# Residual added inside the second FFN product, the first product's last block in another order, and the final norm by halves of the tokens, in a one-core float32 decoder layer

## The chip, the core and the metric

The kernel runs on one core of a Trainium2 chip. The metric is the device time of one execution in microseconds (us), smaller being better. The core's engines are named as in the profile: PE is TensorE, DVE is VectorE, ACT is ScalarE, POOL is GpSimd and SP is SyncE. Each works through its own queue in order; waits between engines are semaphores. DMAs are issued from the queue of SP, POOL or ACT and land some microseconds later.

## The reference, cut to what matters

The program computes one layer for 512 prompt tokens and 8 sample tokens, T = 520 token columns, with 2048 features and 8192 FFN features, all in float32. The change touches everything from the residual of the mixers on:

```python
    x = x + jnp.einsum('blm,md->bld', mix, p['w_out'][l].astype(x.dtype))
    hf = rms_norm(x, p['norm_ffn'][l])
    ff = jnp.square(jax.nn.relu(jnp.einsum('bld,df->blf', hf, p['w_ff1'][l].astype(x.dtype))))
    x = x + jnp.einsum('blf,fd->bld', ff, p['w_ff2'][l].astype(x.dtype))
...
    y = rms_norm(x, p['norm_final'])
```

`rms_norm` divides by the root of the mean square over the features, plus 1e-6, and multiplies by a vector.

## The kernel before, in words

**Layout.** Features lie on the 128 partitions and the 520 tokens along the free axis. Tokens are taken in two halves of H = 260 columns, here called c0 and c1. One 128x128 weight block times 260 columns in float32 is done as three matmuls: weights and operands are each split into a high part that PE multiplies in its fast 32-bit form and a low rest (high by high, high by low, low by high). For weights ACT makes the high part (`whi`, L1064) and DVE the rest (`wlo`, L1066).

**Stages.** The in-projection, the mixers and the out-projection take until about 583 us of the span. Then comes FFN1, 32 quads (of 2x2 block groups) with 8 blocks along the inner dimension, about 20 us each. Then FFN2, whose inner dimension of 32 operand groups is cut into windows: 44 quads, of which the first eight have 3, 4, 5, 6, 7, 7, 7 and 7 blocks, and the last eight 6, 6, 6, 6, 7, 7, 7 and 7, and then 5, 4, 3 and 2 for the last pair groups in their last window. Each pass over the windows adds onto 16 result tiles, `X`.

**Quads.** A quad needs not eight products of weight halves by token halves but seven, P1, P2, P3, Q4, P5, P6, P7, on sums and differences of weights (DVE, `sums`, L1028, tiles `raw`) and of operands (`T` and `G` tiles). Each product is an item. Items stand in one list: P1 of a quad, P3 of the quad before, P2, Q4 of the quad before, P6, P7, P5. At item k, PE multiplies item k (`product`) and DVE and ACT make the sums and splits of item k+3 (`split_item`, AHEAD = 3). So what DVE or ACT does late for one item stops PE three items on. `after(n, f)` puts a function into a later item.

**FFN1's results.** `ff1_done` turns the products of quad i into the four operands that FFN2 reads for group i (relu, square, sums; `first_hi`, `hi_of`, `lo_of`), and `store` writes their seven tiles to DRAM (`fx<-o`, L906, on POOL's queue). Since FFN1's input operands fill SBUF until P5 of quad 31 is done, `more_operands` loads FFN2's operands (`o<-fx`, L1019, POOL's queue) as tiles come free; `budget` counts those. In the same list of loads stand the 16 tiles of the residual, `X<-x1d` (L1013, POOL's queue): the two `X` tiles of a window are loaded before its operands, and four items later DVE multiplies each with S2 (`scale_x`, L1000), a row of scale factors. Then P1, P2, P3 (L926) and P7, P5, Q4 (L929) of the window add onto them.

**Norms.** `hf_half` forms the FFN input per half block while the out-projection runs; it also squares the tile on ACT and adds the square to a sum on DVE (`square`, L417; `ssum`, L423 and L425). After item 2 of FFN1 a matmul with ones (`side_sum`, L1111) turns these sums into S2. At the end `sq` does the same for the 16 finished tiles of X, `rstd` (L285 to L289) makes the factor with Ln and Exp on ACT and three operations on DVE, per token half, and a loop (L1217, L1218) multiplies each X tile, 520 columns wide, and stores it (16 DMAs, on SP and ACT).

Of the kernel before, what the change touches and what calls it, by code (L numbers as in the profile page):

```python
# [5 lines left out]
F32 = mybir.dt.float32  # L6
# [60 lines left out]
def trunk_kernel(tc, xT, vecs, w_in, w_out, w_ff1, w2, ca_st, h0_st, cb_st, gate_w, sgu_wT, sgu_b,  # L67
# [4 lines left out]
    with ExitStack() as es:  # L72
# [258 lines left out]
        class Quad:  # L331

            __slots__ = ("src", "q", "op", "done", "raw", "ps", "idx")

            def __init__(self, src, q, op, done, idx):
                self.src, self.q, self.op, self.done, self.idx = src, q, op, done, idx
                self.raw, self.ps = {}, {}
# [485 lines left out]
        def hf_half(j, e):  # L823
# [5 lines left out]
            add = square(x, 2 * j + e)  # L829
            nc.sync.dma_start(x1d[m], x[:, :T])  # L830
            o = hfo[j]
            if e == 0:
# [4 lines left out]
                add()  # L837
            else:
# [11 lines left out]
                add()  # L850
# [12 lines left out]
        def ff1_done(q, p):  # L863
# [7 lines left out]
            elif p == "P5":  # L871
# [39 lines left out]
        nsq = [0]  # L911

        def sq(x):
            n = nsq[0]
            nsq[0] += 1

            def f():
                after(1, square(x, n))
            after(1, f, "a")

        def ff2_done(q, p):
            assert ("X", 2 * q.idx) in flags and ("X", 2 * q.idx + 1) in flags
            a, b = X[2 * q.idx][0], X[2 * q.idx + 1][0]

            def add(o, x):
                V.tensor_tensor(out=o, in0=o, in1=x, op=ALU.add)  # L926

            def sub(o, x):
                V.tensor_tensor(out=o, in0=o, in1=x, op=ALU.subtract)  # L929
            if p == "P1":  # L930
                add(a[:, :H], q.ps["A"])
            elif p == "P2":
                add(a[:, :H], q.ps["B"])
            elif p == "P7":
                sub(b[:, H:], q.ps["D"])
            elif p == "P5":
                after(1, lambda: sub(b, q.raw["u"][:, :T]))
            elif p == "P3":
                add(a[:, H:], q.ps["A"])
                if q.done:  # L940
                    sq(a)
            elif p == "Q4":
                sub(b[:, :H], q.ps["D"])
                if q.done:
                    sq(b)

        for i in range(32):
            quads.append(Quad([w_ff1[(2 * i + r) * 2 + c] for r in (0, 1) for c in (0, 1)], 8, hfo, None, i))
# [3 lines left out]
        for n, (i, a, b) in enumerate(WIN):  # L952
            src = w2[off:off + 4 * 128 * 128 * (b - a)].rearrange("(j p c) -> j p c", j=4, p=128)
            quads.append(Quad(src, b - a, ffo[a:b], b == 32, i))
# [3 lines left out]
        NQ = len(quads)  # L958
        for n in range(NQ + 1):
            q0, q1 = (quads[n - 1] if n else None), (quads[n] if n < NQ else None)  # L960
            for q, p in ((q1, "P1"), (q0, "P3"), (q1, "P2"), (q0, "Q4"), (q1, "P6"), (q1, "P7"), (q1, "P5")):
                if q is not None:
                    items.append((q, p))
        NU = NP + len(items)
        first_use = {}
        for k, (q, p) in enumerate(items):
            first_use.setdefault(q, NP + k)
# [3 lines left out]
        for q in quads:  # L971
            wloads += [(first_use[q], q, j) for j in ("w11", "w12", "w21", "w22")]

        def more_weights():
            while wloads and len(rfree) > 1:
# [6 lines left out]
                else:  # L982
                    r = q.raw[j] = raw_tile()
# [5 lines left out]
        for n, (i, a, b) in enumerate(WIN):  # L989
            if 0 < n < 8:  # L990
                oloads += [(None, 2 * i), (None, 2 * i + 1)]
            for g in range(4):
                oloads += [(k, g) for k in range(had, b)]
                if n == 0 and g == 0:
                    oloads += [(None, 0), (None, 1)]
# [3 lines left out]
        def scale_x(m):  # L999
            V.tensor_tensor(out=X[m][0], in0=X[m][0], in1=S2[0], op=ALU.mult)  # L1000
            flags.add(("X", m))

        def more_operands():
            while oloads:
                k, g = oloads[0]
                n = 2 if k is not None and g else 1
                if n > budget[0]:
# [293 lines left out]
```

## Time and profile before

| what | value |
| --- | --- |
| median of 3 runs | 1945.11 us (1943.94 to 1945.44) |
| the profiled execution | 1945.04 us, of which span 1943.3 us |
| PE busy over the span | 1881.3 us (97%) |
| DVE, ACT, POOL busy | 1565.1 (81%), 971.1 (50%), 255.7 (13%) us |
| TensorE clock granted, mean over the span | 0.985 of full speed |
| DMA over the span | 330.70 MB, 170 GB/s |

The span is the time from the first to the last event that the profile shows, and 1.7 us lie outside it. "Busy" counts instructions that an engine executes; idle time is put down to the event that ended it (`<-` names the engine, line and tile that released it). The granted clock stands as a share: 1.00 is 2.4 GHz and 0.50 is 1.2 GHz. Times in the rows count from the span's start.

### The profile page before, as it was taken

The page shows a single profiled execution, that of the slowest core. Times are in us where ns is not written, and L with a number is a line of the kernel's source. Part 1 is how long each engine was busy: PE and PEld are TensorE (multiplying, and loading weights), DVE is VectorE, ACT ScalarE, POOL GpSimd, SP SyncE. Part 2 cuts the span into 40 slices and gives each one's busy share as a digit, 9 for nine tenths or more (in the row PEclk, how much of TensorE's full clock was granted, in tenths as well). Part 3 has the DMA queues.
Part 4 walks back from the last instruction along what each step waited for, and adds up shares of the span by engine and source line. Part 5 has one row for each costly group of instructions (what it writes and reads, how often), then busy time and mean ns, then how long its engine had stood idle before and what let it go on. Part 6 is the DMA issues. An engine that isn't in the chain of part 4 may idle for free.

```text
span 1943.3 us, 37918 instructions
## 1 busy us (share of the span) xinstructions
PE 1881.3 (97%) x15532; PEld 1875.4 (97%) x15532; DVE 1565.1 (81%) x2187; ACT 971.1 (50%) x1423; POOL 255.7 (13%) x483
## 2 busy tenths in 40 slices
PE   8999999999999999999999999679999999999994
PEld 8999999999999999999999999679999999999993
DVE  7878777564788888888888888588788888888887
ACT  7444444552345666666666666334444444444443
POOL 0000000000000121211212122620321202212000
PEclk9999999999999999999999999889999999999997
DMA  6223123134344565555655556873764746647322
GB/s 248 104 93 118 68 93 112 59 137 148 106 152 141 182 208 197 197 207 182 213 192 201 203 187 227 321 244 106 257 216 140 260 150 223 212 145 266 119 75 99
DMA packets 108334, 330.70 MB, mean 170 GB/s; under 512 B 16128, under 2 KB 20352, under 8 KB 108160
## 3 DMA queue, kind: packets, MB, share of 16 engines
q1 hardware_dynamic: 69744, 202.45, 31.4%
q0 software_dynamic: 37120, 123.57, 17.7%
q8 instruction: 122, 2.00, 0.4%
q10 hardware_dynamic: 1296, 2.26, 0.3%
q14 instruction: 52, 0.43, 0.1%
HBM read 259.34 MB, written 68.87 MB: 169 GB/s over the span
## 4 chain that ended last, share of the span: by engine, by line
PE 94%; DVE 2%; POOL 1%; issue 1%; DMA 1%; ACT 1%; SPq 0%; DVEq 0%; POOLq 0%; ACTq 0%
PE psA L1084 12%; PE psA L1087 12%; PE psA L1086 12%; PE ps L181 9%; PE ps L179 9%; PE ps L177 9%; PE psD L1086 6%; PE psD L1084 6%; PE psD L1087 6%; PE psB L1087 3%; PE psB L1086 3%; PE psB L1084 3%; DMA X<-x1d 1%; POOL o L1019 1%; DVE X L1217 1%
## 5 line engine op out<-in xcount | busy, mean ns | idle before, releaser
L1064 ACT ACTIVATE whi<-raw 128x1024 fp32r<-128x1024 f32 (+6 forms) x532 | 489.6, 922 | 358.7 <-PE psD L1086 149.4
L1066 DVE TENSOR_TENSOR wlo<-raw,whi 128x1024 fp32r<-128x1024 f32 (+6 forms) x532 | 560.1, 1053 | 100.7 <-ACT whi L1064 99.3
L1084 PE MATMUL psA<-o,whi 128*128 128x260 f32 x2048 | 581.0, 284 | 10.0 <-ACT z L1101 5.6
L1087 PE MATMUL psA<-o,wlo 128*128 128x260 f32 x2048 | 581.3, 284 | 1.7 <-DVE wlo L1066 1.7
L1086 PE MATMUL psA<-o,whi 128*128 128x260 f32 x2048 | 580.7, 284 | 0.0
L1084 PEld LDWEIGHTS psA<-o,whi 128*128 128x128 f32 x2048 | 388.6, 190 | 11.2 <-ACT z L1101 6.0
L1087 PEld LDWEIGHTS psA<-o,wlo 128*128 128x128 f32 x2048 | 388.3, 190 | 2.0 <-DVE wlo L1066 1.9
L1086 PEld LDWEIGHTS psA<-o,whi 128*128 128x128 f32 x2048 | 388.2, 190 | 0.0
L1028 DVE TENSOR_TENSOR raw<-raw,raw 128x1024 f32<-128x1024 f32 (+6 forms) x304 | 319.3, 1050 | 11.1 <-DMA raw<-w 11.0
L177 PE MATMUL ps<-Ah,whi 128*128 128x260 f32 x1536 | 311.1, 284 | 6.1 <-ACT Ah L354 6.1
L179 PE MATMUL ps<-Al,whi 128*128 128x260 f32 x1536 | 310.3, 284 | 0.0
L181 PE MATMUL ps<-Ah,wlo 128*128 128x260 f32 x1536 | 310.0, 283 | 0.0
L1087 PE MATMUL psD<-o,wlo 128*128 128x260 f32 x1024 | 290.4, 284 | 16.2 <-DVE wlo L1066 16.2
L1086 PE MATMUL psD<-o,whi 128*128 128x260 f32 x1024 | 290.7, 284 | 0.8 <-DMA o<-fx 0.8
L1084 PE MATMUL psD<-o,whi 128*128 128x260 f32 x1024 | 290.5, 284 | 0.5 <-DMA o<-fx 0.5
L177 PEld LDWEIGHTS ps<-Ah,whi 128*128 128x128 f32 x1536 | 238.2, 189 | 6.6 <-ACT Ah L354 6.4
L181 PEld LDWEIGHTS ps<-Ah,wlo 128*128 128x128 f32 x1536 | 237.9, 189 | 0.0
L179 PEld LDWEIGHTS ps<-Al,whi 128*128 128x128 f32 x1536 | 237.1, 189 | 0.6 <-DVE Al L357 0.6
L906 POOL DMA_DIRECT2D fx<-o x224 | 121.8, 544 | 836.2 <-DVE o L792 591.1
L1087 PEld LDWEIGHTS psD<-o,wlo 128*128 128x128 f32 x1024 | 193.7, 189 | 16.6 <-DVE wlo L1066 16.6
L1086 PEld LDWEIGHTS psD<-o,whi 128*128 128x128 f32 x1024 | 193.5, 189 | 1.0 <-DMA o<-fx 1.0
L1084 PEld LDWEIGHTS psD<-o,whi 128*128 128x128 f32 x1024 | 193.5, 189 | 0.7 <-DMA o<-fx 0.7
(196 smaller groups left out, 2267.0 us busy)
## 6 DMA issues: line engine op xcount, KB each, us to landing
raw<-w_ff SPq DMA_DIRECT2D x128, 512.0 KB, 4.1
fx<-o POOLq DMA_DIRECT2D x224, 260.0 KB, 3.4
o<-fx POOLq DMA_DIRECT2D x224, 260.0 KB, 4.6
raw<-w SPq DMA_DIRECT2D x116, 384.0 KB, 3.7
raw<-w_in SPq DMA_DIRECT2D x62, 512.0 KB, 5.8
raw<-w_out SPq DMA_DIRECT2D x32, 512.0 KB, 5.8
raw<-w SPq DMA_DIRECT2D x32, 448.0 KB, 3.3
M<-xT SPq DMA_DIRECT2D x24, 260.0 KB, 6.2
```

The lines of the kernel that those rows point to most:

```text
L177: PE.matmul(ps[:, h, :H], hi[:, kk], xh[:, h * H:(h + 1) * H], start=st, stop=False)
L179: PE.matmul(ps[:, h, :H], hi[:, kk], xl[:, h * H:(h + 1) * H], start=False, stop=False)
L181: PE.matmul(ps[:, h, :H], lo[:, kk], xh[:, h * H:(h + 1) * H], start=False, stop=sp)
L906: P.dma_start(fxd[i][2 * g - 1 + n if g else 0], t[0][:, :].bitcast(F32))
L1019: P.dma_start(t[0][:, :].bitcast(F32), fxd[k][2 * g - 1 + n if g else 0])
L1028: V.tensor_tensor(out=o[0][:, :n], in0=x[0][:, :n], in1=y[0][:, :n], op=ALU.add)
L1064: S.activation(out=whis[i][:, :n], in_=r[0][:, :n], func=AF.Copy)
L1066: V.tensor_tensor(out=wlos[i][:, :n], in0=r[0][:, :n], in1=whis[i][:, :n].bitcast(F32), op=ALU.subtract)
L1084: PE.matmul(ps, hi[:, kk], xh, start=p in ("P1", "P2", "P7") and j == 0, stop=False, skip_group_check=True)
L1086: PE.matmul(ps, hi[:, kk], xl, start=False, stop=False, skip_group_check=True)
L1087: PE.matmul(ps, lo[:, kk], xh, start=False, stop=p in ("P3", "P2", "Q4") and j == q.q - 1, skip_group_check=True)
L1217: V.scalar_tensor_tensor(out=X[m][0], in0=X[m][0], scalar=vc(V_FIN + m), in1=RF, op0=ALU.mult, op1=ALU.mult)
```

## The change

1. **Squares of the residual.** `hf_half` squares nothing any more. Instead `sum_x1`, at P1 of FFN1's quads 2 to 17, loads a residual tile back (POOL's queue, into a `z` tile), squares it on ACT six items later and adds it on DVE seven items later. S2 is made at quad 20 (`make_S2`), where `side_sum` now multiplies two sources for each half. The weight sums of quad 0 stand one item earlier.
2. **Last quad of FFN1.** Quad 31 (`LAST1`) runs P1, P6, P5, P2, P7, P3, Q4 to its end before the first window starts; before, its P3 and Q4 stood among the first window's products.
3. **Residual inside FFN2.** The first eight windows load no residual: the `X` tiles begin with a copy of the products (ACT for P1 and P3, DVE's `neg` for P5 and Q4, an add for P2). `add_x1` brings the residual in windows 8 to 23, one tile in each: POOL loads it into a `z` tile at P1, DVE multiplies it with S2 seven items later and adds it to `X` eight items later. Operand loads are held until 14 items before use.
4. **Last four quads (`late`).** Their P2 and Q4, eight products, move behind all others, and the two weight tiles are loaded a second time. Squares and their sums go by token halves. Products after `H1_DONE` touch c0 alone, so that c1's norm (`last_norm(1)`) is started two items into them, three result tiles per item; c0's follows after the last product.
5. **Norm.** A Sqrt on ACT (its table set loaded at P1 of the first late quad, `add_eps`) and a `reciprocal` on DVE take the place of Ln and Exp. The three further operations stay. The results are multiplied and stored as half tiles: 32 operations and 32 DMAs in place of 16.

The core of the diff:

```diff
@@ hf_half
-            add = square(x, 2 * j + e)
...
-                add()
+        def sum_x1(m):
+
+            z = later_x1(m)
...
+            after(6, lambda: S.activation(out=z, in_=z, func=AF.Square), "a")
+            after(7, lambda: V.tensor_tensor(out=ssum[m % 2], in0=ssum[m % 2], in1=z, op=ALU.add))
+        def add_x1(m):
+            z = later_x1(m)
+            after(7, lambda: V.tensor_tensor(out=z, in0=z, in1=S2[0], op=ALU.mult))
+            after(8, lambda: V.tensor_tensor(out=X[m][0], in0=X[m][0], in1=z, op=ALU.add))
...
+            def neg(m, sl, x, y):
+                V.scalar_tensor_tensor(out=X[m][0][:, sl], in0=x, scalar=-1.0, in1=y, op0=ALU.mult, op1=ALU.subtract)
+            if q.win < 8:
+
+                if p == "P1":
+                    X[ma], X[mb] = place(F32, "X"), place(F32, "X")
+                    budget[0] -= 2
+                    S.activation(out=X[ma][0][:, c0], in_=q.ps["A"], func=AF.Copy)
...
             if p == "P1":
+                add(ma, c0, q.ps["A"])
+                if q.win < 24:
+                    add_x1(ma if q.win < 16 else mb)
...
             elif p == "P7":
+                sub(mb, c1, q.ps["D"])
+                if q.late:
+                    sub(mb, c0, q.ps["D"])
...
+                seq = [(q1, "P1"), (q0, "P3"), (q1, "P6"), (q0, "Q4"), (q1, "P5"), (q1, "P2"), (q1, "P7"),
+                       (q1, "P3"), (q1, "Q4")]
...
+        H1_DONE = len(items)
+        items += [(q, p) for q in quads if q.late for p in ("P2", "Q4")]
...
-                if k is None:
-                    X[g] = place(F32, "X")
-                    P.dma_start(X[g][0], x1d[g])
-                    after(4, lambda g=g: scale_x(g))
-                    continue
...
+        def last_norm(h):
...
+            ps, = side_sum(*fsum, halves=(h,))
+            z, o = Zt()[:, sl], RF[0][:, sl]
+            S.activation(out=z, in_=ps, func=AF.Sqrt, scale=1.0 / D)
+            V.reciprocal(o, z)
...
+            for m in range(16):
+                x = X[m][0][:, sl]
+                V.scalar_tensor_tensor(out=x, in0=x, scalar=vc(V_FIN + m), in1=o, op0=ALU.mult, op1=ALU.mult)
+                (S if m % 2 and not h else nc.sync).dma_start(yT[m][:, sl], x)
+                if m % 3 == 2:
+                    yield
...
+                if i - NP == H1_DONE + 2:
+                    fin = last_norm(1)
+                if i - NP >= H1_DONE + 2:
+                    next(fin, None)
```

POOL's queue around P5 of FFN1's quad 31, before. `fx<-o` are stores of operands of groups 30 and 31, `o<-fx` loads of the first window's operands, `X<-x1d` loads of the residual:

```order
L906 DMA fx_768<-o_14945 128x520
L906 DMA fx_769<-o_15022 128x520
L1019 DMA o_15163<-fx_567 128x520
...
L1019 DMA o_15191<-fx_578 128x520
L1019 DMA o_15192<-fx_579 128x520
L1013 DMA X_15195<-x1d_785 128x520
L906 DMA fx_770<-o_15097 128x520
L906 DMA fx_771<-o_15126 128x520
L1013 DMA X_15253<-x1d_786 128x520
L1019 DMA o_15255<-fx_580 128x520
```

The same place of the changed kernel:

```order
L905 DMA fx_768<-o_14965 128x520
L1094 DMA o_15103<-fx_574 128x520
L1094 DMA o_15104<-fx_575 128x520
...
L1094 DMA o_15131<-fx_580 128x520
L1094 DMA o_15133<-fx_581 128x520
L1094 DMA o_15134<-fx_582 128x520
L905 DMA fx_769<-o_15040 128x520
L1094 DMA o_15250<-fx_583 128x520
L1094 DMA o_15251<-fx_584 128x520
```

Before, 16 operand loads stand behind the store of `fx_769`, and residual loads stand between the loads and stores that follow. Now 17 operand loads, the rest of the first window, stand ahead of that store, and there are no residual loads.

DVE's queue where the out-projection ends, before. `raw` are the weight sums of FFN1's quad 0, `wlo` the low rest of a weight tile, `ssum` the sums of squares; the block that begins with L1161 (`M` or `T` plus a product) forms one tile of the residual and the operands from it:

```order
L800 TENSOR_TENSOR o_6931<-g_6917,o_6925 128x520
L423 TENSOR_TENSOR ssum_6038<-ssum_6038,z_6914 128x520
L1028 TENSOR_TENSOR raw_6934<-raw_6640,raw_6644 128x1024
L1028 TENSOR_TENSOR raw_6644<-raw_6644,raw_6711 128x1024
L1066 TENSOR_TENSOR wlo_6938<-raw_6642,whi_6937 128x1024
L1161 TENSOR_TENSOR M_769_5248<-ps_6941,M_769_5248 128x520
```

The same place of the changed kernel, one unit later in its weight sums:

```order
L802 TENSOR_TENSOR o_6894<-g_6880,o_6888 128x520
L1101 TENSOR_TENSOR raw_6611<-raw_6615,raw_6611 128x1024
L1147 TENSOR_TENSOR wlo_6898<-raw_6613,whi_6897 128x1024
L1271 TENSOR_TENSOR M_769_5248<-ps_6901,M_769_5248 128x520
```

The add to `ssum` is gone, and one of the two weight sums has moved a unit earlier.

DVE's queue at the end of the changed kernel, from the last `wlo` of all to the reciprocal of c0's norm. L974 and L978 add products to X, L955 adds half squares to the sums, L1223 multiplies c1 halves of X with the norm's factor:

```order
L1147 TENSOR_TENSOR wlo_23531<-raw_23406,whi_23530 128x256
L974 TENSOR_TENSOR X_15592<-X_15592,psB_23535 128x260
L1223 SCALAR_TENSOR_TENSOR X_15442<-X_15442,vec,RF 128x260
L1223 SCALAR_TENSOR_TENSOR X_15592<-X_15592,vec,RF 128x260
...
L955 TENSOR_TENSOR fsum_22393<-fsum_22393,z_23583 128x260
L955 TENSOR_TENSOR fsum_22452<-fsum_22452,z_23600 128x260
L1223 SCALAR_TENSOR_TENSOR X_16553<-X_16553,vec,RF 128x260
L1216 RECIPROCAL RF<-z_23615 128x260
```

Before, eight operations stood between the last `wlo` and the first operation of the norm, and all 16 multiplications of X behind it. Now 22 stand there, 13 of them multiplications of c1.

## Rows read from the trace of the kernel before

**Rows 1.** Stretches: busy PE, PEld, DVE, ACT, POOL (instructions); clock granted; DMA share; GB/s.

```profile
583.00:631.60 48.60, 46.68 (x369) 45.95 (x368) 42.51 (x52) 27.04 (x41) 3.94 (x7) 0.96 0.41 141
...
1214.60:1263.10 48.50, 32.00 (x227) 30.72 (x225) 25.29 (x48) 16.45 (x31) 30.62 (x56) 0.84 0.88 321
1263.10:1311.70 48.60, 38.66 (x280) 37.92 (x281) 40.48 (x62) 17.38 (x27) 12.14 (x23) 0.85 0.71 245
1311.70:1360.30 48.60, 48.60 (x409) 48.60 (x408) 38.98 (x49) 20.46 (x25) 0.00 (x0) 1.00 0.35 106
...
1894.70:1943.30 48.60, 20.98 (x157) 19.36 (x156) 35.56 (x70) 19.43 (x36) 0.00 (x0) 0.76 0.27 99
```

**Rows 2.** Waits from 1205 to 1320 us: total, times, longest.

```profile
DVE X L1000 <- DMA X<-x1d: 21.2, 5, 6.6
...
PE psD L1087 <- DVE wlo L1066: 16.2, 2, 12.0
...
DVE raw L1028 <- DMA raw<-w: 4.7, 2, 4.6
...
PE psA L1084 <- ACT z L1101: 3.9, 1, 3.9
```

**Rows 3.** POOL's timeline: start, duration, instruction; idle before it in brackets.

```profile
1220.16 0.54 POOL L906 DMA_DIRECT2D fx<-o  x1 [8.85 <-DVE o L792]
1220.77 5.74 POOL L1019 DMA_DIRECT2D o<-fx  x10
```

**Rows 4.** DMA issues from 1205 to 1290 us: count, size, median us to landing.

```profile
o<-fx POOLq DMA_DIRECT2D x51, 260.0 KB, 5.1
...
X<-x1d POOLq DMA_DIRECT2D x14, 260.0 KB, 6.1
...
raw<-w SPq DMA_DIRECT2D x4, 320.0 KB, 7.1
```

**Rows 5.** DVE's lines from 1205 to 1320 us: count, busy us, mean ns, idle before.

```profile
L1000 DVE TENSOR_TENSOR X<-X,S 128x520 f32<-128x520 f32 x16 | 10.6, 697 | 21.2 <-DMA X<-x1d 21.2
```

**Rows 6.** A stretch of 2 us inside the second stall, columns as in rows 1.

```profile
1268.00:1270.00 2.00, 2.00 (x10) 1.87 (x9) 2.00 (x5) 0.80 (x2) 1.71 (x4) 0.50 0.94 320
```

**Rows 7.** Timelines of DVE and PE where the out-projection ends.

```profile
576.22 0.69 DVE L423 TENSOR_TENSOR ssum<-ssum,z 128x520 f32<-128x520 f32 x1
...
582.73 0.69 DVE L423 TENSOR_TENSOR ssum<-ssum,z 128x520 f32<-128x520 f32 x1
...
590.05 1.31 DVE L800 TENSOR_TENSOR o<-g,o 128x520 fp32r<-128x520 f32 x2
```

```profile
590.19 0.39 PE L1086 MATMUL psB<-o,whi 128*128 128x260 f32 x1 [0.70 <-DVE o L800]
```

**Rows 8.** The timeline from the last low rest of a weight to the end.

```profile
1913.03 0.42 DVE L1066 TENSOR_TENSOR wlo<-raw,whi 128x256 fp32r<-128x256 f32 x1
...
1919.39 1.96 PE L1111 MATMUL side<-ssum,ones 128*128 128x260 f32 x4 [3.52 <-DVE ssum L1211]
1920.57 1.28 ACT L285 ACT_TABLE_LOAD   x1 [2.98 <-PE side L1111]
1921.86 0.39 ACT L285 ACTIVATE z<-side 128x260 f32<-128x260 f32 x1
...
1924.47 0.43 DVE L288 SCALAR_TENSOR_TENSOR z<-z,RF 128x260 f32<-128x260 f32 x1
1924.94 0.43 DVE L289 SCALAR_TENSOR_TENSOR RF<-z,RF 128x260 f32<-128x260 f32 x1
...
1928.84 10.82 DVE L1217 SCALAR_TENSOR_TENSOR X<-X,vec,RF 128x520 f32<-128x520 f32 x16
```

**Rows 9.** Busy time from the last four quads' first product on, columns as in rows 1.

```profile
1872.60:1912.80 40.20, 38.53 (x321) 38.24 (x319) 36.01 (x71) 21.86 (x43) 0.00 (x0) 1.00 0.19 54
```

**Rows 10.** The only reciprocal on DVE, and a plain operation of its shape: shortest, median, longest ns.

```profile
L440 DVE RECIPROCAL sp<-sp x1: 202/202/202, 27.0 to 27.0; 128x8 f32<-128x8 f32 x1
```

```profile
L442 DVE TENSOR_TENSOR sp<-sp,sp x1: 159/159/159, 27.4 to 27.4; 128x8 f32<-128x8 f32 x1
```

More of the change, by code (lines that the diff above doesn't have):

```diff
@@ new lines, in trunk_kernel, with sq, add @@
+        c0, c1, both = slice(0, H), slice(H, T), slice(0, T)
+        fsum = [None, None]
+        def sq(m, sl):
+            n, x = m % 2, X[m][0]
+            if fsum[n] is None:
+                fsum[n] = cp.tile([128, T], F32, tag=f"ssum{n}", name=nm("fsum"))
+                after(1, lambda: S.activation(out=fsum[n], in_=x, func=AF.Square), "a")
+                return
+            z = Zt()
+            def add():
+                V.tensor_tensor(out=fsum[n][:, sl], in0=fsum[n][:, sl], in1=z[:, sl], op=ALU.add)
@@ L917, in f, with add_eps @@
             def f():
-                after(1, square(x, n))
+                S.activation(out=z[:, sl], in_=x[:, sl], func=AF.Square)
+                after(1, add)
             after(1, f, "a")
+        def add_eps():
+            z = Zt()
+            S.activation(out=cp.tile([128, 1], F32, name="warm"), in_=ones[:, 0:1], func=AF.Sqrt)
+            S.activation(out=z, in_=S2[0], func=AF.Square)
+            after(1, lambda: V.scalar_tensor_tensor(out=fsum[0], in0=z, scalar=EPS * D / 128, in1=fsum[0],
+                                                    op0=ALU.mult, op1=ALU.add))
@@ L936, in ff2_done, with u @@
             elif p == "P5":
[L937 removed]
+                def u():
+                    sub(mb, both, q.raw["u"])
+                    if q.late:
+                        sq(mb, c1)
+                after(1, u)
             elif p == "P3":
[L939 removed]
+                add(ma, c1, q.ps["A"])
                 if q.done:
[L941 removed]
+                    sq(ma, c1 if q.late else both)
             elif p == "Q4":
[L943 removed]
+                sub(mb, c0, q.ps["D"])
@@ L944, in ff2_done @@
                 if q.done:
-                    sq(b)
+                    sq(mb, c0 if q.late else both)
         for i in range(32):
-            quads.append(Quad([w_ff1[(2 * i + r) * 2 + c] for r in (0, 1) for c in (0, 1)], 8, hfo, None, i))
+            quads.append(Quad([w_ff1[(2 * i + r) * 2 + c] for r in (0, 1) for c in (0, 1)], 8, hfo, i))
         off = 0
@@ L982, in more_weights @@
                 else:
+                    assert j not in q.raw
                     r = q.raw[j] = raw_tile()
@@ L988, in trunk_kernel @@
         had = 0
[L989 to L995, printed above, removed]
+        for q in quads[32:]:
+            i, a, b = WIN[q.win]
+            for g, p in enumerate(("P1", "P2", "P6", "P7")):
+                oloads += [(q.pos[p], k, g) for k in range(had, b)]
             had = max(had, b)
         budget = [0]
-        def scale_x(m):
-            V.tensor_tensor(out=X[m][0], in0=X[m][0], in1=S2[0], op=ALU.mult)
-            flags.add(("X", m))
         def more_operands():
             while oloads:
-                k, g = oloads[0]
-                n = 2 if k is not None and g else 1
-                if n > budget[0]:
+                at, k, g = oloads[0]
+                n = 2 if g else 1
+                if n > budget[0] or NP + at > it[0] + 14:
                     break
@@ L1077, in product @@
             b = BANK[p]
-            if p in ("P1", "P2", "P7"):
+            first = p in ("P1", "P2", "P7") or (q.late and p == "Q4")
+            if first:
                 q.ps[b] = ps2[0].tile([128, H], F32, tag=b, name=nm(f"ps{b}"), bufs=2)
```

172 lines of the change are left out of this document (104 added, 68 removed).

## The prediction, made before the changed kernel ran

> **What bounds the kernel now.** I read the stretches of equal length first, to see where PE is not full. In a full stretch of 48.6 us PE issues 409 matmuls at the full granted clock, 0.119 us each, and DVE is busy about 39 of the 48.6 us [rows 1]. So PE is the bound, and only places where it falls short can give time back. There are three.
>
> The largest is the change from FFN1 to FFN2. The stretches at 1214.6 and 1263.1 hold 227 + 280 = 507 matmuls [rows 1]. These are 507 x 0.119 = 60.2 us of work in 97.1 us: **36.9 us are lost**, 26.4 as idle PE and the rest at half clock, which the rows show inside the stall (0.50 while PE is busy throughout [rows 6]). Then I read the waits of that place. DVE waits five times, 21.2 us in all, for a residual tile `X<-x1d` to land, and PE waits 16.2 us in two pieces for `wlo` and 3.9 us for an ACT copy [rows 2]. DVE works in order: the `wlo` that PE lacks stand behind `scale_x` in DVE's queue, so the same lateness is counted on both engines. The tiles are late because POOL's queue is late: it stands 8.85 us before a store, until 1220.16, and ten operand loads only then follow [rows 3], with DMA engines busy 0.88 of the stretch after that [rows 1].
>
> The second is the end of the out-projection: 369 matmuls where 409 fit [rows 1], so 40 x 0.119 = 4.8 us lost. PE is idle for 1.9 of them (46.68 busy of 48.60), waiting for DVE's chain that ends with L800 at 590.05 [rows 7]; some 0.9 are S2's matmuls (half of the 1.96 us that four such records take at a low clock [rows 8]); the rest is a granted clock below 1.00.
>
> The third is the end: after the last `wlo` at 1913.03 PE has little left, and from PE's matmul with ones at 1919.39 to the span's end at 1943.3 it takes 23.9 us [rows 8].
>
> **Part 1, squares out of the out-projection.** Two adds to `ssum` stand in the chain that ends at 590.05, 0.69 us each [rows 7], and one weight sum moves a unit earlier, half of a pair whose 1024 columns cost about 1.2 us each. The chain is then 2.5 to 3 us earlier. PE's idle of 1.9 us there goes, one piece of it 0.70 [rows 7], and with it the low clock behind it, about 1.5 us. At quad 20 S2's matmuls come back with twice as many: I take 1.8 us there against 0.9 before. Net gain 3.4 - 0.9 = **2.5 us**, bounds 1 (half of the idle stays) and 3.8 (all lost time goes).
>
> The squares themselves become one more ACT operation and one more DVE operation of 0.69 us in each 20-us quad, 1.7 us in a stretch where DVE has some 6 us free [rows 1]. I cost them at nothing. If that cover were gone, 16 x 0.69 = 11 us would show.
>
> **Parts 2 and 3, the middle.** What is removed: 16 `scale_x`, 10.6 us of DVE [rows 5], all of DVE's 21.2 us of waiting for them [rows 2], and 14 residual tiles that stood among 51 operand loads [rows 4]. What is moved: 17 operand loads now stand ahead of the store at which POOL waited until 1220.16 [rows 3], and most go into tiles already free, so they can start some 9 us earlier. And quad 31's last products no longer share items with the first window, so that window starts about 5 us later and has its 21 tiles by then: POOL issued ten loads in 5.74 us [rows 3], landing takes about 5 us [rows 4].
>
> What is late next? Three things, each with a row. The raw weights: DVE waited 4.6 us once for a tile [rows 2], at 7.1 us landing [rows 4]; that traffic is lighter now but not gone, so I take 2.5 us. ACT: copies of P1 and P3 into X free a PSUM bank, and they queue behind group 31's relu and squares; PE waited 3.9 us for such a copy before [rows 2], and I take 2 us. DVE: group 31's assembly still falls among the small windows, 1 us. The clock: 10.5 us of the 36.9 before went with 26.4 us of idle, so 5.5 us of idle bring some 1.5 us. Together 7 us, a gain of **30 us**. The bounds: nothing remains late (gain 36.9), or only the 21.2 us that DVE waited for residuals comes back (gain 21). I am nearer to the first since the PE waits of 16.2 and 3.9 us both lie behind DVE or ACT work that the residual held up.
>
> In windows 8 to 23 DVE gets two operations of about 0.69 us in each window of some 15 us, 4.5 us in a stretch in which it is busy 39 of 48.6 [rows 1], and POOL one load. Cover is there again; without it, 32 x 0.69 = 22 us. The multiplication waits seven items behind the load's issue, about 15 us, where the same tiles took 6.1 us under the heaviest traffic [rows 4].
>
> **Parts 4 and 5, the end.** Here I balance DVE, not PE. Before, from 1872.6 to the matmul with ones at 1919.39 are 46.8 us, DVE busy 36.0 in the first 40.2 [rows 9] and about 5.4 in the rest: 41.4. The change adds to this: sixteen half sums (0.43) for eight whole ones (0.69), +1.4; four more subtractions, +1.7; and the c1 norm: a reciprocal, three operations 0.47 us apart [rows 8], and 16 half multiplications. A whole one takes 10.82/16 = 0.68 us [rows 8], a half between 0.34 and 0.47; I take 0.40, 6.4 us. One addition (0.7) goes. The reciprocal has one row: 202 ns on 8 columns where a plain operation takes 159 [rows 10]. That is 43/8 = 5.4 ns more for each column, so with 1 ns for the plain part 1.8 us for 260 columns. Its bounds are 0.47, as the other three, and 260/8 x 202 ns = 6.6. Sum +11.5: DVE then has 52.9 us of work in a piece that took 46.8, and it becomes the bound of the last four quads. With 1 to 2 us in which it waits for PE, the last sum stands near 1927, some 7.5 us later than before.
>
> Behind it the tail is shorter: matmul 1.1, Sqrt 0.4, reciprocal 1.8, three operations 1.4, sixteen halves 6.4, the last store 3.6 (before: 1943.3 less the end of L1217 at 1939.7 [rows 8]), hops 0.2: 14.9 us against 23.9, 9 us less. The four table loads of 1.28 us that stood in line there, the first at 1920.57 [rows 8], are out of it, 5.1 us of the nine. Net gain 9 - 7.5 = **1.5 us**. The bounds: with a reciprocal of 0.47 us and halves of 0.34 it is 2 x 1.3 + 32 x 0.06 = 4.5 more, gain 6; with one of 6.6 us it is 2 x 4.8 = 9.6 less, a loss of 8.
>
> The next ACT instruction begins at 1921.86, 0.01 us after the table load of 1.28 us ends [rows 8]. The Trainium skill, "ScalarE: Activation LUTs", section "What ACT_TABLE_LOAD costs", gives some 1.28 us for the load and another 1.38 us to drain for each switch; the load agrees, the drain does not show in this trace. By the page the four would free 5.5 us more, and the gain at the end would be 7.
>
> The reciprocal costs 5.4 ns a column beyond a plain operation [rows 10]. The Trainium skill, "VectorE: DVE Perf Modes", section "First, the fixed hardware budget", says that it is an iterative divide with a repeat count of 8; eight times a plain half of 0.34 us would be 2.7 us, an estimate by that page, and the gain at the end would fall to about -0.3.
>
> **The sum.** 2.5 + 30 + 1.5 = 34 us off the profiled execution's 1945.04 us, which lies 0.07 us from the median of 1945.11: 1911 us.
>
> **Rivals.**
> (a) The middle stays partly stalled: POOL's loads and the raw weights still fill the DMA engines (0.71 to 0.88 in those stretches [rows 1]) or ACT's copies hold PSUM. For it: PE also waited on these before [rows 2]. Against: the longest waits all lead to the residual. The loss is then 16 to 22 us instead of 7, the time 1920 to 1926.
> (b) The end gains 6 us or more: a cheap reciprocal and a DVE that keeps up. Time 1903 to 1907. For it: only one row of 8 columns speaks for a dear one.
> (c) The end loses: a reciprocal near 6.6 us in DVE's queue ahead of the `wlo` that PE needs. Time near 1921. Against: the row shows only 43 ns more.
> (d) Slower than before. The residual's wait is not removed but moved: in windows 8 to 23 DVE's multiplication with S2 waits for its `z` tile as `scale_x` waited for X, with `wlo` behind it. Sixteen waits; from 34/16 = 2.1 us of PE time each it decides. At 4.6 us, the size of most of the five [rows 2], it is 74 us, 1985 us. Against it: landing would have to exceed about 15 us, and where windows run undisturbed DMA engines are busy 0.35 [rows 1].
> (e) The change does not act: the stall in the middle was only named after X, and operands or weights arrive no earlier. Gains and losses of the ends cancel, and the time is within 0.2%, 3.9 us, of before, which is about what a measurement of this kernel can tell from no change. Against: DVE's idle is on X alone.
>
> **How the numbers follow.** The forecast, 1907 to 1919, 0.60; (a) 0.15; (b) 0.13; (c) 0.06; (d) 0.03; (e) 0.01; 0.02 for faster still. The range takes the forecast, most of (a) and (b) and all of (c): 1902 to 1925. Faster by over 0.2%: all but (d) and (e), 0.96; within 0.2%: 0.01; slower: 0.03.
>
> **What the profile after would show.** Right: DVE has no wait for a residual tile between 1205 and 1300, and both stretches there together lose 5 to 10 us; the stretch at 583 holds some 390 to 400 matmuls; DVE is busy without a gap over the last 20 us before c0's norm, and the span ends some 15 us behind the last sum. Wrong: DVE idle on `z<-x1d` in windows 8 to 23; PE in the middle waiting over 10 us for `o<-fx`, for `wlo` behind a raw weight, or for an ACT copy; a reciprocal far from 1.8 us.

## The result and the profile after

The changed kernel takes **1910.44 us** (median of 4 runs, 1909.63 to 1910.74) where the kernel before takes 1944.55 on the same chips: a ratio of 0.9824, with a 95% interval of 0.9807 to 0.9841. The forecast was 1911. The profiled execution took 1910.32 us, its span is 1908.6 us.

The same stretches as in [rows 1] (busy PE, PEld, DVE, ACT, POOL; clock granted; DMA share; GB/s), and the last 48.6 us:

```profile
583.00:631.60 48.60, 48.60 (x408) 48.60 (x407) 41.14 (x51) 28.36 (x43) 5.04 (x10) 1.00 0.46 159
...
1214.60:1263.10 48.50, 44.38 (x361) 43.35 (x360) 33.19 (x61) 26.08 (x51) 28.46 (x52) 1.00 1.01 374
1263.10:1311.70 48.60, 47.39 (x392) 46.97 (x392) 39.48 (x46) 21.45 (x31) 3.28 (x6) 1.00 0.52 180
...
1860.00:1908.60 48.60, 25.56 (x185) 23.26 (x184) 42.11 (x99) 15.90 (x38) 0.00 (x0) 0.78 0.42 135
```

The start of FFN1 is now a full stretch, 408 matmuls where 369 stood [rows 1]. The two stretches of the middle hold 753 matmuls where 507 stood, at a granted clock of 1.00. At 409 in a full stretch, 817 would fit: 64 are missing, 64 x 0.119 = 7.6 us, where 36.9 us were lost before. PE is idle for 5.3 of the 7.6 (4.1 and 1.2); the rest shows in no wait.

What DVE and PE wait for from 1205 to 1320 us (total, times, longest), to be held against [rows 2]:

```profile
DVE raw L1101 <- DMA raw<-w: 12.8, 5, 4.2
...
PE psA L1170 <- DVE wlo L1147: 2.8, 2, 1.8
...
PE psB L1170 <- DVE wlo L1147: 2.0, 2, 1.7
```

No residual tile is waited for any more. What is left is weight tiles, which landed about as slowly as before (6.8 us, 7.1 in [rows 4]) while the DMA engines were busy throughout (1.01 in the stretch above). The DMA issues from 1205 to 1290 us (count, size, median us to landing), as in [rows 4]:

```profile
o<-fx POOLq DMA_DIRECT2D x51, 260.0 KB, 5.8
...
raw<-w SPq DMA_DIRECT2D x4, 320.0 KB, 6.8
```

The end, in DVE's timeline: the reciprocal of c1's norm, the last `wlo`, the last half sums, the reciprocal of c0's norm and its 16 multiplications, to be held against [rows 8]:

```profile
1879.77 1.78 DVE L1216 RECIPROCAL RF<-z 128x260 f32<-128x260 f32 x1 [0.93 <-ACT z L1215]
...
1885.41 0.42 DVE L1147 TENSOR_TENSOR wlo<-raw,whi 128x256 fp32r<-128x256 f32 x1
...
1892.91 0.75 DVE L955 TENSOR_TENSOR fsum<-fsum,z 128x260 f32<-128x260 f32 x2
...
1895.99 1.78 DVE L1216 RECIPROCAL RF<-z 128x260 f32<-128x260 f32 x1 [1.93 <-ACT z L1215]
...
1899.20 6.49 DVE L1223 SCALAR_TENSOR_TENSOR X<-X,vec,RF 128x260 f32<-128x260 f32 x16
```

DVE works without a gap from the first of these rows to the last sum's end at 1893.66. From that end to the span's end are 14.9 us. Before, from the end of DVE's last operation ahead of the matmul with ones, at 1919.33, they were 24.0.

### The profile page after: what moved, and what is told of

Its sections match the earlier page's. It is cut to its first block, busy times and chain, and to the rows that moved or that the text cites. A ratio compares the mean times of both kernels' runs of the same rounds, so it can differ in the third digit from the quotient of the medians.

```text
span 1908.6 us, 38079 instructions
## 1 busy us (share of the span) xinstructions
PE 1874.4 (98%) x15540; PEld 1869.0 (98%) x15540; DVE 1563.5 (82%) x2206; ACT 968.5 (51%) x1443; POOL 264.0 (14%) x499
## 4 chain that ended last, share of the span: by engine, by line
PE 95%; DVE 2%; DMA 1%; issue 1%; POOL 1%; ACT 0%; SPq 0%; DVEq 0%; POOLq 0%; ACTq 0%
PE psA L1167 12%; PE psA L1170 12%; PE psA L1169 12%; PE ps L181 10%; PE ps L179 10%; PE ps L177 10%; PE psD L1169 6%; PE psD L1167 6%; PE psD L1170 6%; PE psB L1170 3%; PE psB L1167 3%; PE psB L1169 3%; DVE X L1223 1%; DVE wlo L1147 0%; DMA raw<-w 0%
## 5 line engine op out<-in xcount | busy, mean ns | idle before, releaser
L1145 ACT ACTIVATE whi<-raw 128x1024 fp32r<-128x1024 f32 (+5 forms) x532 | 488.9, 921 | 327.5 <-PE psD L1169 143.1
L1147 DVE TENSOR_TENSOR wlo<-raw,whi 128x1024 fp32r<-128x1024 f32 (+5 forms) x532 | 558.8, 1051 | 88.2 <-ACT whi L1145 86.7
```

The lines of the kernel that those rows point to most:

```text
L1145: S.activation(out=whis[i][:, :n], in_=r[0][:, :n], func=AF.Copy)
L1147: V.tensor_tensor(out=wlos[i][:, :n], in0=r[0][:, :n], in1=whis[i][:, :n].bitcast(F32), op=ALU.subtract)
```

## Experiments

Times are medians; each run is held against the changed kernel's 1910.44 us unless it says otherwise. "Matmuls" are those of a stretch as above. The kernel before, measured again beside each group of runs, had medians from 1944.09 to 1944.68 us and single executions up to 2 us from them, so a difference of 1 to 2 us between two runs here is near the noise.

### The middle: which of three edits broke the stall

**Quad 31's old order** (part 2 undone, and the weight sums of quad 31 and of the first window at their usual places):

```diff
-            if q1 is LAST1:
+            if False:
...
-            elif p == ("P7" if i == 31 else "P5"):
+            elif p == "P5":
```

> The changed kernel with part 2 undone: quad 31's P3 and Q4 stand among the first window's products again, its weight sums as every quad's. Theory (the residual tiles in POOL's and DVE's queues made the stall, the order only lets the operand loads start earlier): 3 to 15 us slower than the changed kernel, 1914 to 1925 us, PE waiting for o<-fx or for wlo at the first window, no wait for a residual. Rival (the order made the gain): over 20 us slower, above 1930 us, with a PE wait of over 8 us in one piece.

Measured: 1911.74 us (1910.89 to 1912.97), 1.3 us slower. PE's longest wait there was 3.0 us. With the rest of the change in place, the order is worth less than either view had it.

**The residual back in the first eight windows** (part 3 undone; loads, `scale_x` and adds as before, no `add_x1`):

```diff
+                if k is None:
+                    X[g] = place(F32, "X")
+                    P.dma_start(X[g][0], x1d[g])
+                    after(4, lambda g=g: scale_x(g))
+                    continue
...
-                if q.win < 24:
-                    add_x1(ma if q.win < 16 else mb)
```

> The changed kernel with part 3 undone: the two residual tiles of a window are loaded ahead of its operands and multiplied with S2 four items later, as before, the first eight windows add to them, and windows 8 to 23 add no residual; quad 31's new order, the limit of 14 items and the rest stay. Theory: DVE waits for X again, 10 to 21 us in all, and the time is 1922 to 1937 us. Rival (the order of quad 31 and the earlier start of the operand loads made the gain, the residual tiles come in time once POOL does not stand behind a store): at most 1915 us, DVE waiting less than 4 us for X.

Measured: 1920.41 us (1919.67 to 1922.4), 10.0 us slower, between the two forecasts. DVE's waits on X came back (its waits from 1190 to 1320 us: total, times, longest):

```profile
DVE X L1086 <- DMA X<-x1d: 14.1, 3, 6.0
```

Yet the two stretches hold 261 + 405 matmuls, 159 more than before. With the residual in its old place more than half of the gain was still there, and the new order, worth 1.3 us in the run above, hardly explained it. So I undid both.

> The changed kernel with parts 2 and 3 both undone: quad 31's old order and the residual tiles loaded and scaled in the first eight windows, as before; only the limit of 14 items on operand loads is left of the change there. Either one undone alone gave back 1.9 us (order) and 10.5 us (residual) of the 29.3 us that the middle gained. Theory (the two stand in for each other: POOL behind a store and the residual tiles in the same queue make the stall together, and either taken away breaks it): 24 to 29 us slower than the changed kernel, 1934 to 1940 us, DVE waiting 18 us or more for X. Rival 1 (their shares add): 12 to 13 us slower, 1922 to 1924 us. Rival 2 (the limit on operand loads carries the rest): likewise 1922 to 1926 us, with DVE waiting for X as in the run with the residual alone back, some 14 us.

Measured: 1923.38 us (1922.2 to 1923.97), 12.9 us slower. My theory that the two stand in for each other fell: the shares nearly add (1.3 + 10.0 = 11.3), and some 16 us of the middle's gain remained with neither. Of part 3's and part 2's code in the middle one condition was left: `or NP + at > it[0] + 14`, the limit on how early an operand is loaded.

**The limit alone, put into the kernel before** (the list of loads then carries the item of first use, `at`, for operands and residual tiles alike):

```diff
-                if n > budget[0]:
+                if n > budget[0] or at > it[0] + 14:
```

> The kernel before with one edit: operand and residual loads of FFN2 are held until 14 items before use. With quad 31's order and the residual both put back, the changed kernel still kept some 15.7 of the 29.3 us that the middle gained. Theory (the limit carries them: the program places scale_x four items behind its load, so a load that is written earlier than POOL can issue it puts scale_x on DVE ahead of weight sums that PE needs sooner; held loads put it later): 13 to 17 us faster than before, 1927 to 1931 us, DVE waiting 10 to 15 us for X instead of 21.2, and none of its waits after the second window. Rival (something else in that run carries them, the tiles of the later squares or the earlier start of FFN1): within 4 us of before, 1940 to 1945 us.

Measured: 1928.18 us (1926.36 to 1929.0) against 1944.46, **16.3 us faster by this condition**, a ratio of 0.9915 (0.9902 to 0.9929). DVE's wait for X from 1205 to 1320 us (total, times, longest), and its timeline of `scale_x`:

```profile
DVE X L1001 <- DMA X<-x1d: 11.0, 3, 6.3
```

```profile
1237.95 0.70 DVE L1001 TENSOR_TENSOR X<-X,S 128x520 f32<-128x520 f32 x1 [6.33 <-DMA X<-x1d]
...
1245.78 0.70 DVE L1001 TENSOR_TENSOR X<-X,S 128x520 f32<-128x520 f32 x1 [4.42 <-DMA X<-x1d]
1246.72 0.70 DVE L1001 TENSOR_TENSOR X<-X,S 128x520 f32<-128x520 f32 x1 [0.25 <-DMA X<-x1d]
1258.23 1.31 DVE L1001 TENSOR_TENSOR X<-X,S 128x520 f32<-128x520 f32 x2
1271.74 1.31 DVE L1001 TENSOR_TENSOR X<-X,S 128x520 f32<-128x520 f32 x2
```

The last two rows are the fourth and the fifth window: from there on DVE waits for X no more (I had expected it one window earlier), and PE's 12.0-us wait for `wlo` [rows 2] is gone: the longest that PE waits for a `wlo` there is 1.0 us. The limit holds operand loads back too, but the weights did not come earlier by that: DVE's waits for `raw<-w` rose from 4.7 [rows 2] to 6.1 us. The kernel before, in DVE's timeline for the same two windows and in POOL's for the fourth window's two loads:

```profile
1257.71 1.37 DVE L1000 TENSOR_TENSOR X<-X,S 128x520 f32<-128x520 f32 x2 [4.68 <-DMA X<-x1d]
1263.71 1.37 DVE L1000 TENSOR_TENSOR X<-X,S 128x520 f32<-128x520 f32 x2 [4.63 <-DMA X<-x1d]
```

```profile
1251.11 0.55 POOL L1013 DMA_DIRECT2D X<-x1d  x1
1251.84 0.55 POOL L1013 DMA_DIRECT2D X<-x1d  x1 [0.18 <-issue]
```

These tiles do not come earlier with the limit: POOL starts to issue the fourth window's two at 1251.20 (before 1251.11) and the fifth's at 1265.62 (before 1259.33). They are asked for later. The reason stands in DVE's program, before and with the limit, at the same place:

```
before:
L800 TENSOR_TENSOR o_15440<-g_15251,o_15425 128x520
L1000 TENSOR_TENSOR X_15345<-X_15345,S_7182 128x520
L1000 TENSOR_TENSOR X_15347<-X_15347,S_7182 128x520
L1000 TENSOR_TENSOR X_15363<-X_15363,S_7182 128x520
L1000 TENSOR_TENSOR X_15365<-X_15365,S_7182 128x520
L929 TENSOR_TENSOR X_14935<-X_14935,z_15391 128x520
L1028 TENSOR_TENSOR raw_15216<-raw_15303,raw_15216 128x512
L1066 TENSOR_TENSOR wlo_15449<-raw_15052,whi_15448 128x384

with the limit:
L800 TENSOR_TENSOR o_15412<-g_15251,o_15397 128x520
L929 TENSOR_TENSOR X_14935<-X_14935,z_15355 128x520
L1029 TENSOR_TENSOR raw_15216<-raw_15299,raw_15216 128x512
L1067 TENSOR_TENSOR wlo_15417<-raw_15052,whi_15416 128x384
```

The kernel before writes a residual load into the program as soon as `budget` allows, and `scale_x` four items behind it. POOL's queue is then far behind, so those four items have passed on DVE long before the tile lands, and DVE stands in front of a `wlo` of the first window for four tiles of the fourth and fifth. With the limit the fourth window's `scale_x` stands behind four more `wlo`, the fifth's later still.

**The limit at 9 items instead of 14:**

> The changed kernel with one number changed: operand loads are held until 9 items before use, not 14. In the changed kernel PE still idles some 5 us in the middle for weight tiles that land 6 to 7 us after issue, while DMA engines are busy without a gap from 1218 to 1274 us. Theory (operand loads that are not yet needed crowd out the weights): DVE waits less for raw<-w, 12.8 us falls to under 8, and the time is 2 to 4 us lower, 1906.5 to 1908.5 us. Rival (the tiles come free at the same times and the same bytes have to move, or operands then come late): within 1 us of the changed kernel or slower, PE waiting for o<-fx.

Measured: 1912.98 us (1911.2 to 1914.06), 2.5 us slower; DVE waited 12.4 us for `raw<-w`, as with 14. The rival's first half holds: a tighter limit does not bring the weights earlier. What makes them late among 71 transfers of 260 KB was not tested by taking transfers away.

Where the 2.5 us went is another matter. The two stretches of the middle hold 362 + 393 = 755 matmuls, as many as with 14. The profile loses them later: 4150 matmuls from 1360 to 1860 us, where the changed kernel has 4172. The run with only the weight sums back (below), whose edit does not reach that piece, has 4152 there. So the limit of 9 is not shown to cost anything.

### The start of FFN1

**The squares back in the out-projection** (part 1 undone, the weight sums of quad 0 left one unit early):

```diff
+            add = square(x, 2 * j + e)
...
-                if 2 <= q.idx < 18:
-                    sum_x1(q.idx - 2)
```

> The changed kernel with part 1 undone: hf_half squares the residual again, S2 is made at item 2 of FFN1, nothing is done at quads 2 to 17 and 20; the weight sums of quad 0 stay one item early. Theory (the two adds to ssum in DVE's chain are what stopped PE there): quad 1 of FFN1 starts 2.5 to 4.7 us later than in the changed kernel, the 1.8 us at quad 20 come back, so 1911 to 1913.5 us; the 48.6-us stretch at 583 holds 375 to 390 matmuls. Rival (the weight sum that moved one unit earlier made the gain): the stretch keeps 400 or more matmuls and the time is 1908.5 to 1910, below the changed kernel, since only the 1.8 us at quad 20 go.

**Only the weight sums back:**

```diff
-                    at = (max(o["P1"] - 1, 0), o["P1"], o["P2"], o["P6"])
+                    at = (o["P2"], o["P2"], o["P6"], o["P6"])
```

> The changed kernel with only the weight sums of FFN1's quad 0 put back, two with P2 and two with P6, a unit later; the squares stay out of the out-projection. With the squares put back instead, FFN1 started 1.5 us later, 0.9 of it S2's two matmuls. Theory after that run (most of the 4.7 us at the start of FFN1 came from the weight sums' place): FFN1's quad 5 starts 3.0 to 3.4 us later than in the changed kernel, the stretch at 583 holds 375 to 385 matmuls, the time is 1913 to 1914.5 us. Rival (either of the two edits is enough): under 1 us later.

The stretch at 583 of the first run, and then of the second (columns as above):

```profile
583.00:631.60 48.60, 47.76 (x394) 47.35 (x394) 43.04 (x55) 27.86 (x43) 3.94 (x7) 1.00 0.46 152
```

```profile
583.00:631.60 48.60, 47.63 (x396) 47.22 (x395) 42.05 (x52) 28.37 (x42) 4.49 (x8) 1.00 0.48 158
```

Squares back: 14 matmuls fewer than the changed kernel, 1.7 us, though S2's four records now count among the 394. This lies between the 375 to 390 of the theory and the 400 of its rival. The run took 1910.57 us (1909.32 to 1911.95), the same as the changed kernel, since the eight records at quad 20 are gone. Sums back: 12 fewer, 1.4 us, not the 3 us that I expected after the first; 1912.84 us (1910.89 to 1914.55), 2.4 us slower, but its profile loses 20 matmuls, 2.4 us, between 1360 and 1860 us as well, where this edit does nothing. PE's waits from 560 to 640 us say more than these counts. Before, they were 0.8 us for an ACT copy, 0.7 for L800 and 0.4 for an operand from ACT. With either edit alone only the 0.8 is left, and with both nothing. So each of the two ends the wait for DVE's chain and the 0.4, and the last 0.8 us takes both. Moving the squares as a whole brought nothing that the time shows: what it saves at the start it pays at quad 20, as PE's timeline of the changed kernel shows:

```profile
983.03 1.91 PE L1202 MATMUL side<-ssum,ones 128*128 128x260 f32 x8
```

The stretch of the kernel before is itself not exact: with the limit as only edit, which changes nothing there, it held 382 matmuls in place of 369, with the same idle time of PE (1.9 us) and a granted clock of 1.00 in place of 0.96.

### The end

**The old end** (parts 4 and 5 undone; all four quads in the usual order, Ln and Exp, whole tiles):

```diff
-n >= 8 * (len(ENDS) - 1)))
+False))
...
+            rstd(ps, RF[:, sl], z[:, sl], 1.0 / D)
```

> The changed kernel with parts 4 and 5 undone: the last four quads in the usual order, squares of whole tiles, Ln and Exp, 16 whole multiplications and 16 stores at the end. Theory (the new tail is 8 to 9 us shorter, but DVE's half-width work ahead of it gives 6 to 7 back): 2 to 3 us slower than the changed kernel, 1912.5 to 1913.5 us; the last sum some 6 us earlier, the tail behind it 24 us. Rival (the end is worth the whole tail): 1917 to 1920 us.

Measured: 1914.57 us (1912.7 to 1915.59), 4.1 us slower, above the 2 to 3 expected and below the rival. In the profile DVE's last operation ahead of the matmul with ones ended at 1889.33 us (the changed kernel: 1893.66), 24.1 us ahead of the span's end (14.9). Counted from the same `wlo` of 896 columns in both programs (it starts at 1837.94 here, at 1837.09 in the changed kernel), this operation comes 5.2 us later in the changed kernel.

**Ln and Exp in the new order:**

```diff
-            S.activation(out=z, in_=ps, func=AF.Sqrt, scale=1.0 / D)
-            V.reciprocal(o, z)
+            S.activation(out=z, in_=ps, func=AF.Ln, scale=1.0 / D)
+            S.activation(out=o, in_=z, func=AF.Exp, scale=-0.5)
```

> The changed kernel with its norm factor made by Ln and Exp on ACT, as before, in place of Sqrt and the reciprocal; halves and late products stay. By rows (a table load 1.28 us, Ln 0.39, Exp 0.42, against Sqrt 0.39 and a reciprocal 1.78 on DVE): the tail behind the last half sum is 1.2 us longer, and c1's factor takes some 1.2 us more, of which DVE idles through 3 to 4 us instead of 0.9: 1.5 to 3 us slower, 1912 to 1913.5 us. Rival (each switch also drains for 1.38 us, as the Trainium skill, ScalarE: Activation LUTs, section What ACT_TABLE_LOAD costs, has it): 5 us or more on top, 1917 us or above, with gaps of over 1 us behind the loads.

Measured: 1911.6 us (1911.01 to 1913.22), 1.2 us slower, a little less than the 1.5 to 3 expected; the span of the profiled execution, the slowest of the four, is 1911.1 us, 2.5 us longer. ACT's timeline at c0's norm:

```profile
1896.85 1.28 ACT L1214 ACT_TABLE_LOAD   x1 [3.27 <-PE side L1201]
1898.15 0.39 ACT L1214 ACTIVATE z<-side 128x260 f32<-128x260 f32 x1
1898.55 1.28 ACT L1215 ACT_TABLE_LOAD   x1
1899.85 0.42 ACT L1215 ACTIVATE RF<-z 128x260 f32<-128x260 f32 x1
```

Each load is followed by its ACTIVATE within 0.02 us, and the second load follows the ACTIVATE ahead of it as closely. The rival, the drain of 1.38 us that the Trainium skill states ("ScalarE: Activation LUTs", section "What ACT_TABLE_LOAD costs"), shows neither in the rows nor in the time; the load of 1.28 us agrees.

**c1's multiplications off DVE**, first all 16, then every second one:

```diff
+                if h:
+                    S.activation(out=x, in_=x, func=AF.Copy, scale=vc(V_FIN + m))
+                    P.tensor_tensor(out=x, in0=x, in1=o, op=ALU.mult)
```

> The changed kernel with the 16 multiplications of c1's norm taken off DVE: ACT multiplies a tile with the weight vector and POOL with the row of factors. Theory (DVE's half-width work bounds the last four quads): the last half sum comes 5 to 6.4 us earlier, PE no longer waits for wlo there, and the time is 4 to 6 us lower, 1904.5 to 1906.5 us. Rival (POOL is slower than DVE by so much, or slows DVE down where both read SBUF, that c1's results end last or the sums come no earlier): within 1 us of the changed kernel or slower.

> The changed kernel with two edits: every second tile of c1's norm is multiplied by ACT and POOL in place of DVE, and S2's sums are added on DVE before two matmuls, not four. With all 16 tiles on POOL (0.80 us each) DVE's own operations beside them took up to 0.95 us for 0.42, and ACT's 16 scalings stood ahead of the squares. Theory: half of them leaves DVE 3 us less and POOL busy for 6.4 us instead of 12.7, and S2 gains 0.9 us: 1905.5 to 1907.5 us, at or below the run with all on POOL (1907.8). Rival (POOL and DVE share the way to SBUF, so whatever POOL does DVE loses): 1908.5 to 1910 us.

Measured: all 16, 1907.83 us (1907.43 to 1908.6), **2.6 us faster**, between the 4 to 6 of the theory and its rival; every second one, 1910.9 us (1910.13 to 1911.63), no gain, nearer to its rival. Counted from the `wlo` named above, DVE's last half sum ended 1.9 us earlier than in the changed kernel in the first run (5 to 6.4 expected) and 0.4 us later in the second. The timelines of POOL and of DVE in the run with all 16:

```profile
1883.39 12.72 POOL L1225 TENSOR_TENSOR X<-X,RF 128x260 f32<-128x260 f32 x16 [119.02 <-DVE RF L1219]
```

```profile
1883.50 0.95 DVE L1147 TENSOR_TENSOR wlo<-raw,whi 128x256 fp32r<-128x256 f32 x1
1884.37 0.41 DVE L978 TENSOR_TENSOR X<-X,psD 128x260 f32<-128x260 f32 x1
1884.71 0.63 DVE L955 TENSOR_TENSOR fsum<-fsum,z 128x260 f32<-128x260 f32 x1
```

POOL's 16 products end to end, and three of DVE's rows beside them. While POOL multiplies, DVE's operations on two SBUF tiles take 0.95 and 0.63 us for 0.42, and the one that reads PSUM keeps its 0.41. DVE's own multiplications, 0.41 to 0.43 us each in the changed kernel, took up to 0.64 in the second run, as its timeline has it:

```profile
1887.29 0.62 DVE L1228 SCALAR_TENSOR_TENSOR X<-X,vec,RF 128x260 f32<-128x260 f32 x1
```

I read from this that a tile on POOL pays only if it leaves DVE little else of that kind to do; two runs do not prove it. The Trainium skill, "GPSIMD Engine Reference", section "1. Specifications", says that POOL shares its way to SBUF with DVE and contends with DVE instructions that have two SBUF inputs; the trace agrees: the operation with one operand in PSUM is spared.

The second run's other edit, adding S2's sums on DVE ahead of two matmuls, failed too: PE waited for the add, as PE's timeline of that run shows.

```profile
983.41 1.12 PE L1203 MATMUL side<-ssum,ones 128*128 128x260 f32 x4 [1.04 <-DVE ssum L932]
```

**Both repaired** (all 16 on POOL, ACT's scalings spread, the add a quad earlier):

```diff
+                elif q.idx == 19:
+                    V.tensor_tensor(out=ssum[0], in0=ssum[0], in1=ssum[1], op=ALU.add)
...
+            if h:
+                scale(6)
```

> The changed kernel with all 16 tiles of c1's norm multiplied on POOL, ACT's scalings spread so that six come ahead of the norm's factor and two with each step (in the first such run three in a row held up the squares), and S2's sums added on DVE a whole quad ahead of two matmuls (in the run with half the tiles on POOL the add stood right ahead of them and PE waited for it). Theory: the last half sum comes 1 us earlier than in the first run with all tiles on POOL, S2 gives 0.9 us: 1905.5 to 1907.0 us. Rival (the squares wait for DVE's adds and not for ACT, and DVE's slow operations beside POOL set the end): 1907 to 1908.5 us.

Measured: **1906.82 us** (1905.89 to 1908.34), the fastest of all: 0.9803 of the kernel before (0.979 to 0.9817). It is 1.0 us below the first run with all tiles on POOL, and the two ranges overlap. The last half sum, counted as above, ended 0.7 us earlier than there; S2's matmuls take 1.04 us in PE's timeline in place of 1.91, with no wait:

```profile
982.12 1.04 PE L1204 MATMUL side<-ssum,ones 128*128 128x260 f32 x4
```

## Why the prediction was right, and where it was not

**The sum** held: 34 us were forecast and 34.1 measured (1944.55 - 1910.44). That it held so closely is luck. By the runs the middle gave 29.2 us (16.3 + 12.9; 30 forecast) and the end 4.1 (1.5 forecast), which leaves 0.8 for FFN1's start (2.5 forecast): the misses cancel. And half of the middle was right for a reason that I had not seen.

**The middle, 30 us: size right, cause half seen.** The loss that remains is 7.6 us (7 forecast). But the step "What is removed" gave the whole gain to the residual's 21.2 us of waiting on DVE and to POOL's earlier start, and the limit of 14 items had no term at all. The runs, taken in this order, give: the limit 16.3 us, put alone into the kernel before; then taking the residual out 10.0 us (11.6 with the old order: 1923.38 - 1911.74) and the new order 1.3 us (3.0 without part 3: 1923.38 - 1920.41). In another order the shares may differ: the residual moved out without the limit was not run. A kernel with no `scale_x` in the first windows has none to place too early, so there the limit may be worth little; that is open. What is shown is that I had read the waits on X as "the tiles are late", while half of them (21.2 us fell to 11.0) were "DVE asks too early", which a later place in the program cures though the loads are issued no earlier. The rows would have shown it: four `scale_x` stand in a row in DVE's program ahead of a `wlo` of the first window. I looked at POOL's queue there and not at DVE's.

**What is late next.** The raw weights were sized too low (2.5 us forecast; PE waited 2.8 + 2.0 for `wlo` behind them), ACT's copies too high (2 us; PE waited 0.4 for one), and the clock that I charged 1.5 us (by the ratio that I used, 10.5 to 26.4, it is 2.2) stayed at 1.00 in both stretches.

**FFN1's start: 2.5 us, too high or about right.** The stretch became full, 39 matmuls or 4.6 us more than in one profile of the old start and 26 or 3.1 us more than in the other; less the 1.9 us at quad 20 (1.8 forecast) that is 2.7 or 1.2 us, and the runs leave 0.8. My upper bound of 3.8 did not take off the matmuls at quad 20 in full: 4.8 - 1.8 is 3.0. I put PE's 1.9 us of idle down to L800 alone, where 0.7 was that wait and 1.2 lay with ACT. That the squares and the weight sums stand in one chain was right; that moving the squares pays is not shown: with it undone the time was the same.

**The end, 1.5 us: 4.1 by the run with the old end.** The prices were right: a reciprocal of 1.78 us (1.8, from a row of 8 columns), halves of 0.41 us (0.40), a tail of 14.9 us (14.9). What was off is the term for DVE's backlog. Counted from the same `wlo`, the sums were ready 5.2 us later than in the run with the old end, not 7.5. DVE's busy time from there grew by 9.2 us (44.3 to 53.5), not 11.5, and the operations that I listed even add up to 12.0. A part of the difference is that half operations end to end start 0.34 us apart in DVE's timeline, where I counted 0.43 for sums and subtractions. DVE did work without a gap in the last 14 us, and taking 16 operations off it did move the end. The estimate by the Trainium skill's repeat count of 8 for the divide ("VectorE: DVE Perf Modes", section "First, the fixed hardware budget"), 2.7 us, was too high; the small row was the better source.

**The rivals.** (a) did not come: the middle's rest was 7.6 us, near the 7. (b) and (c) did not come, the reciprocal being where its row put it. (d) did not come: DVE has no wait for `z<-x1d` in the whole run. The changed kernel's DMA issues from 1340 to 1570 us (count, size, median us to landing):

```profile
z<-x1d POOLq DMA_DIRECT2D x16, 260.0 KB, 3.8
```

The tiles landed in 3.8 us, and PE shows no wait at all in that time, so the two operations that each window got cost nothing in this profile. But the room became smaller: DVE's waits for `raw<-w` from 1330 to 1870 us are 16.1 us, where before they were 6.3 and in the run with the residual back 5.1. In the two profiles that lose 20 and 22 matmuls there they are 25.8 and 24.6. (e) fell with the result.

## What to carry to other kernels

When an engine waits for a transfer, ask two questions: why the transfer is late, and why the engine asks for it there. An instruction placed a fixed number of steps behind the issue of its load, on an in-order engine that has other work, turns a late queue into a stall of everything behind it; placing it by its use took one condition here and, alone, gave 16.3 us. And a change with several parts is not explained by a sum that comes out: here it did, with one part unpriced, one that the time does not show and one that gave more than twice its forecast, and only undoing the parts one at a time showed it.

## What the runs showed that I had not expected

- POOL next to DVE: 0.80 us for a product of 128x260, and DVE's operations on two SBUF tiles slowed from 0.42 to between 0.62 and 1.01 us, while those with an operand in PSUM stayed at 0.41.
- Sums of squares that leave a busy chain can cost as much elsewhere: eight records of a float32 matmul with ones are 1.9 us of PE, and four, with the two sums added first, 1.04.
- The same code ran the start of FFN1 with 369 matmuls in one execution and 382 in another, a difference of 1.5 us, so a gain of that size there is not told from one profile.
